# Two more PSUM banks and a longer belt in the stick-breaking attention of a three-block model

## The chip, the cores and the metric

The kernel runs on one core of a Trainium2 chip. The engines are TensorE (PE, with its weight loads shown apart as PEld), VectorE (DVE), ScalarE (ACT), GpSimd (POOL) and SyncE (SP, which issues the DMAs). The metric is the time of one execution in microseconds on the device, the median of several runs.

## What is computed

Three transformer-like blocks in a row over 1024 tokens of width 1024, in fp32. The change is in the third block, in one of its two attentions. It has 8 heads of width 64. A query at t weights the key at s < t by a sigmoid of its score, times the product of the complements of all keys between them ("stick breaking"):

```python
z = jnp.einsum('bhqd,bkhd->bhqk', qb, k) * scale
log_beta = jax.nn.log_sigmoid(z)
log_1m_beta = jnp.where(causal, jax.nn.log_sigmoid(-z), 0.0)
suffix = lax.cumsum(log_1m_beta, axis=3, reverse=True) - log_1m_beta
attn = jnp.where(causal, jnp.exp(log_beta + suffix), 0.0)
out = jnp.einsum('bhqk,bkhd->bqhd', attn, v)
# then RMS norm, output projection, LayerNorm, gated feed-forward, LayerNorm
```

## The kernel before

Instructions run on each engine in the order in which the program writes them. Waits between engines are semaphores that the framework puts in where a tile is read, or where its buffer is used again. Large matmuls (`qk`, `op`, `dn` and others) run as three matmuls of fp32r halves (hi·hi, hi·lo, lo·hi).

**Items.** The attention takes 128 queries of one head against up to 512 keys as one item. Queries 0 to 511 (`i` 0 to 3) need one item; queries 512 to 1023 (`i` 4 to 7) need two, called segments here: first the keys from 512 on, then keys 0 to 511. That is 12 items a head, 24 for a pair of heads (`p`), 96 in all. An item has three parts:

- `sb1`: scores into a PSUM bank `sb` (PE); two sigmoids from it, `f` and `beta` (ACT); a running product over `f` (the scan of L2156, DVE), a fix-up of one column of `beta`, and, for a first segment, a copy of one column as the `carry` of the second (DVE); `beta` times the shifted `f` (POOL).
- `sb2`: transposes of `beta` into a bank `sbt` (PE), copied out as `pt` (DVE, L2172).
- `sb3`: the products with the values into a bank `sbo` (PE), 64 columns wide, summed over both segments in that bank. After an item that ends its queries the sum is copied out (`ys` or `yr`, DVE, L2184) and squared (`ysq`, ACT). A two-segment sum holds its bank from the first segment's `sb3` to the second's.

**Banks.** [...] One pool `ps` has six of them and gives out a bank for each `sb`, `sbt`, `sbo`, for the projections' sums (`qk`, `op`) and for the transposes of results (`yt`). Two banks are used only by pools of other stages.

**Order.** A `Belt` writes the parts in steps: each step issues the `sb1` of a new item, the `sb2` of the item `lag` steps back, and the `sb3` of an item whose `sb2` is one or two steps old. The `Driver` mixes these steps between the matmuls of a main stream by costs that are written in the code. For the pairs p = 0 to 2, the main stream is the `qk` projection of the next pair: six matmuls, a part of a step, six matmuls, and so on. When the projections are done (around 2257 us), steps are issued without a main stream (`fsb.until`: "forced") until 80 of the 96 items are finished, with the transposes of the other attention's results (`yt`) among them. After that the output projection `op` is the main stream, and `fsb.finish` empties the belt between its two halves.

The work per step on ACT and DVE has this order: ACT `f`, `beta`, then `ysq` of the older item; DVE scan, column of `beta`, `carry`, `pt`, then `ys`.

```python
def _run(self):                       # Belt, each turn is one step
    ...
            ready = [it for n, it in self.end if n < self.n - (0 if force else 1)]
            if self.mid and self.mid[0][0] <= self.n - self.lag:
                it = self.mid.pop(0)[1]
                yield it[1](), 0.0             # sb2
                self.end.append((self.n, it))
            for it in ready:
                cost = it[2]()                 # sb3
```

`tmp` takes `f` and `beta` from a pool of eight buffers (`b3t`) until the forced steps begin, later from the general pool.

Of the kernel before, what the change touches and what calls it, by code (L numbers as in the profile page):

```python
# [9 lines left out]
F32 = mybir.dt.float32  # L10
# [4 lines left out]
PSUM = bass.MemoryType.PSUM  # L15
# [283 lines left out]
class Kernel:  # L299
# [1670 lines left out]
    def block3(self):  # L1970
        nc, a, drv, tc = self.nc, self.a, self.drv, self.tc
        from contextlib import ExitStack
        ctx = ExitStack()
        pp = ctx.enter_context(tc.tile_pool(name="b3", bufs=1))
        tp = ctx.enter_context(tc.tile_pool(name="b3t", bufs=8))
        ctx1 = ExitStack()
        kp = ctx1.enter_context(tc.tile_pool(name="b3k", bufs=4))
        roomy = []
# [64 lines left out]
        def y_put(p, n, e, branch, ssq, write):  # L2043

            own = branch == 0 and p == 3
            if own:
                yc = Y[n][:, 384 + 64 * e:448 + 64 * e]
            else:
                if e == 0:
                    YS[branch, p, n] = self.small(128, "ys")  # L2050
                yc = YS[branch, p, n][:, 64 * e:64 * e + 64]
            write(yc)
            sq = self.small(64, "ysq")
            self.act(sq, yc, AF.Square, accum=ssq[:, n, 2 * p + e:2 * p + e + 1])
            if e == 1 and not own:
                nc.sync.dma_start(out=self.yd[n][:, 512 * branch + 128 * p:512 * branch + 128 * p + 128],
                                  in_=YS.pop((branch, p, n)))
# [71 lines left out]
        def sb_unit(h, i):  # L2129
            nk = 128 * (i + 1)  # L2130
            segs = [(0, nk)] if nk <= 512 else [(512, nk - 512), (0, 512)]
            st = {"n": len(segs)}
            out = []
            for x, (k0, w) in enumerate(segs):
                out.append(((lambda x=x, k0=k0, w=w: sb1(st, h, i, x, k0, w)),
                            (lambda x=x, k0=k0, w=w: sb2(st, h, i, x, k0, w)),
                            (lambda x=x, k0=k0, w=w: sb3(st, h, i, x, k0, w))))
            return out
# [36 lines left out]
        def sb3(st, h, i, x, k0, w):  # L2175
            p, e = h // 2, h % 2
            if x == 0:
                st["po"] = self.bank("sbo")
            po, pt = st["po"], st["pt", x]
            for k in range(w // 128):  # L2180
                self.mm(po[:, 0:64], pt[:, 128 * k:128 * k + 128], V[k0 // 128 + k][:, 64 * h:64 * h + 64],
                        x == 0 and k == 0, x == st["n"] - 1 and k == w // 128 - 1)
            if x == st["n"] - 1:
                y_put(p, i, e, 0, ssb, lambda y: nc.vector.tensor_copy(out=y, in_=po[:, 0:64]))  # L2184
            return 1.7 * w

        fsw, fsb = Belt(drv, 3, 2000.0), Belt(drv, 4, 800.0)

        def q_as(branch, p, half, ps):
            q_evac(p, half, ps)  # L2190
# [96 lines left out]
        def gen_mix(half, b):  # L2287

            n0 = 4 * half
            if not b:  # L2290
                r = self.small(4, "r1")
                token_rms(r, ssb[:, n0:n0 + 4, :])
                ys = Y[n0:n0 + 4]
            else:
                r = rsw[:, n0:n0 + 4]
                ys = [self.h("yr") for _ in range(4)]
                for n in range(4):
                    nc.sync.dma_start(out=ys[n], in_=self.yd[n0 + n][:, 512:1024])
                yield 0.0, 0.0
            for n in range(4):  # L2300
                self.ts(ys[n], ys[n], r[:, n:n + 1])
            yield 0.0, 8470.0
            for c in range(4):
                ps = self.bank("yt")
                for n in range(4):
                    nc.tensor.transpose(ps[:, 128 * n:128 * n + 128], ys[n][:, 128 * c:128 * c + 128], self.ident)
                hi, lo = self.h("hhi", F32R), self.h("hlo", F32R)
                H2[0][c + 4 * b][half], H2[1][c + 4 * b][half] = hi, lo
                g = self.v("swa_norm_g_3" if b else "sb_norm_g_3", c)
                self.act(hi, ps, AF.Identity, scale=g)  # L2310
                self.stt(lo, ps, g, hi, ALU.mult, ALU.subtract)
                yield 450.0, 200.0


        roomy.append(True)
        fsb.lag = 5
        sws = [gen_mix(0, 1), gen_mix(1, 1)]
        next(sws[0])
        next(sws[1])
# [145 lines left out]
```

## Time and profile before

| | |
|---|---|
| median of 3 runs | 3154.49 us (3153.01 to 3156.83) |
| profiled execution | 3154.91 us, span 3153.1 us, mean granted TensorE clock 0.959 |
| busy, share of the span | PE 94%, PEld 80%, DVE 57%, ACT 41%, POOL 45% |
| idle of PE before the span's end | 196 us (3153.1 - 2957.1) |

The span runs from the first to the last instruction, and 1.8 us of the execution's time lie around it. The shares are means over stages that have different limits; the stick-breaking attention is a stage of some 310 us, from 2048 to 2360 us.

### The profile page before, as it was taken

The page shows a single profiled execution, that of the slowest core. Times are in us where ns is not written, and L with a number is a line of the kernel's source. Part 1 is how long each engine was busy: PE and PEld are TensorE (multiplying, and loading weights), DVE is VectorE, ACT ScalarE, POOL GpSimd, SP SyncE. Part 2 cuts the span into 40 slices and gives each one's busy share as a digit, 9 for nine tenths or more (in the row PEclk, how much of TensorE's full clock was granted, in tenths as well). Part 3 has the DMA queues.
Part 4 walks back from the last instruction along what each step waited for, and adds up shares of the span by engine and source line. Part 5 has one row for each costly group of instructions (what it writes and reads, how often), then busy time and mean ns, then how long its engine had stood idle before and what let it go on. Part 6 is the DMA issues. An engine that isn't in the chain of part 4 may idle for free. (4 is left out here: it accounts for less than half of the span.)

```text
span 3153.1 us, 41402 instructions
## 1 busy us (share of the span) xinstructions
PE 2957.1 (94%) x15188; PEld 2514.3 (80%) x15188; DVE 1808.9 (57%) x3522; ACT 1286.6 (41%) x2493; POOL 1429.0 (45%) x1008
## 2 busy tenths in 40 slices
PE   8999998999999999889998989988889899999997
PEld 7898776888878877778897778877678788888886
DVE  6443246666665579966645664566666522224556
ACT  4232224444432254466573356644443422222223
POOL 4313434777743356852214352143333477764330
PEclk9999999999999999999998989989889999999998
DMA  4101241222253221132113332100122222225321
GB/s 159 34 21 54 73 127 41 80 84 81 84 180 107 81 84 51 45 96 60 45 39 104 106 111 64 45 19 22 63 73 94 87 81 81 80 84 177 107 81 54
DMA packets 114876, 248.96 MB, mean 79 GB/s; under 512 B 19696, under 2 KB 31600, under 8 KB 114672
## 3 DMA queue, kind: packets, MB, share of 16 engines
q1 hardware_dynamic: 114384, 246.01, 23.8%
q8 instruction: 120, 1.97, 0.3%
q14 instruction: 84, 0.69, 0.1%
q10 hardware_dynamic: 288, 0.30, 0.0%
HBM read 192.52 MB, written 53.74 MB: 78 GB/s over the span
## 5 line engine op out<-in xcount | busy, mean ns | idle before, releaser
L332 POOL TENSOR_TENSOR wlo<-raw,whi 128x1024 fp32r<-128x1024 f32 x240 | 581.4, 2431 | 861.8 <-ACT whi L326 845.0
L326 ACT ACTIVATE whi<-raw 128x1024 fp32r<-128x1024 f32 x240 | 248.2, 1053 | 537.7 <-PE dn L347 284.0
L332 DVE TENSOR_TENSOR X<-dn,X 128x512 f32<-128x512 f32 (+1 forms) x312 | 209.9, 676 | 161.7 <-PE dn L347 159.5
L347 PE MATMUL dn<-ghi,whi 128*128 128x512 f32 (+1 forms) x736 | 281.4, 382 | 0.6 <-DVE X L332 0.6
L347 PE MATMUL dn<-glo,whi 128*128 128x512 f32 (+1 forms) x736 | 280.6, 381 | 0.0
L347 PE MATMUL dn<-ghi,wlo 128*128 128x512 f32 (+1 forms) x736 | 280.5, 381 | 0.0
L332 POOL TENSOR_TENSOR raw<-raw 128x512 f32<-128x512 f32 x156 | 203.0, 1301 | 12.1
L332 POOL TENSOR_TENSOR slo<-raw,shi 128x512 fp32r<-128x512 f32 x117 | 151.1, 1305 | 105.1 <-ACT shi L326 103.8
L347 PE MATMUL p<-thi,shi 128*128 128x512 f32 x468 | 185.0, 395 | 12.7 <-DVE u L1105 9.4
L332 DVE TENSOR_TENSOR v<-p,e 128x512 f32<-128x512 f32 x78 | 53.8, 690 | 243.2 <-ACT e L326 193.6
L347 PE MATMUL p<-hhi,wlo 128*128 128x512 f32 x468 | 182.4, 390 | 1.7 <-POOL wlo L332 1.7
L347 PE MATMUL p<-tlo,shi 128*128 128x512 f32 x468 | 183.6, 392 | 0.0
L347 PE MATMUL p<-thi,slo 128*128 128x512 f32 x468 | 183.4, 392 | 0.0
L347 PE MATMUL p<-hhi,whi 128*128 128x512 f32 x468 | 182.3, 390 | 0.0
L347 PE MATMUL p<-hlo,whi 128*128 128x512 f32 x468 | 182.3, 390 | 0.0
L329 DVE SCALAR_TENSOR_TENSOR t<-u,vec,t 128x512 f32<-128x512 f32 x176 | 133.0, 755 | 79.7 <-ACT t L326 74.5
L347 PE MATMUL qk<-hhi,whi 128*128 128x512 f32 x384 | 164.9, 430 | 7.9 <-ACT hhi L326 7.2
L332 POOL TENSOR_TENSOR beta<-beta,f 128x511 f32<-128x511 f32 (+3 forms) x96 | 88.4, 925 | 180.7 <-DVE beta L336 177.8
L347 PEld LDWEIGHTS dn<-ghi,whi 128*128 128x128 f32 x736 | 139.3, 189 | 28.0 <-DVE X L332 1.4
L347 PEld LDWEIGHTS dn<-ghi,wlo 128*128 128x128 f32 x736 | 139.1, 189 | 26.3
L347 PEld LDWEIGHTS dn<-glo,whi 128*128 128x128 f32 x736 | 139.2, 189 | 25.8
L347 PE MATMUL qk<-hlo,whi 128*128 128x512 f32 x384 | 156.3, 407 | 1.5 <-DVE hlo L329 1.5
(400 smaller groups left out, 8186.8 us busy)
## 6 DMA issues: line engine op xcount, KB each, us to landing
raw<-in_wall SPq DMA_DIRECT2D x240, 512.0 KB, 3.8
gd<-g SPq DMA_DIRECT2D x88, 256.0 KB, 2.1
gx<-gd SPq DMA_DIRECT2D x88, 256.0 KB, 5.1
x2d<-X SPq DMA_DIRECT2D x64, 256.0 KB, 2.0
X<-x2d SPq DMA_DIRECT2D x64, 256.0 KB, 5.3
x<-in_xT SPq DMA_DIRECT2D x16, 256.0 KB, 5.8
X<-in_xT SPq DMA_DIRECT2D x16, 256.0 KB, 4.3
T<-in_rpbx SPq DMA_DIRECT2D x8, 448.0 KB, 3.6
```

Source lines behind the costliest of these rows:

```text
L326: self.nc.scalar.activation(out=out, in_=in_, func=func, bias=bias, scale=scale, **kw)
L329: self.nc.vector.scalar_tensor_tensor(out=out, in0=in0, scalar=s, in1=in1, op0=op0, op1=op1)
L332: (eng or self.nc.vector).tensor_tensor(out=out, in0=in0, in1=in1, op=op)
L347: self.nc.tensor.matmul(out=out, lhsT=lhsT, rhs=rhs, start=start, stop=stop, skip_group_check=more)
```

## The change

Three numbers and a pool. A pool `po2` of two PSUM banks, on the two that `ps` does not have, holds the output sums of the queries with two segments; the one-segment sums stay in `ps`. The belt's lag is five in place of four, and six in place of five from the forced steps on. The pool of `f` and `beta` has ten buffers in place of eight.

```diff
-        tp = ctx.enter_context(tc.tile_pool(name="b3t", bufs=8))
+        tp = ctx.enter_context(tc.tile_pool(name="b3t", bufs=10))
+        po2 = ctx.enter_context(tc.tile_pool(name="b3p", bufs=2, space=PSUM))
...
             if x == 0:
-                st["po"] = self.bank("sbo")
+                st["po"] = (self.bank("sbo") if st["n"] == 1 else
+                            po2.tile([128, 512], F32, tag="o", name="sbo"))
...
-        fsw, fsb = Belt(drv, 3, 2000.0), Belt(drv, 4, 800.0)
+        fsw, fsb = Belt(drv, 3, 2000.0), Belt(drv, 5, 800.0)
...
         roomy.append(True)
-        fsb.lag = 5
+        fsb.lag = 6
```

Up to the stage's first transposes every engine's instructions stand as before, and no instruction is added or taken away. Inside the stage the order shifts, and waits change.

PE, first pair of heads, at the first output sum `sbo` (names with buffer numbers; the semaphores that a row waits for in brackets). Before:

```order
L2170 MATMUL sbt_18400<-ident_74,beta_18324 128x128 [waits DVE_49,Activation_49,Pool_49]
L347 MATMUL sbo_18404<-v_15723,pt_18361 128x64 [waits DVE_49,Activation_49]
L347 MATMUL sbo_18404<-v_15724,pt_18361 128x64
L347 MATMUL sbo_18404<-v_15725,pt_18361 128x64
L347 MATMUL sbo_18404<-v_15726,pt_18361 128x64
L347 MATMUL sb_18409<-ks_18157,qq_18123 128x384 [waits PE_49]
```

Now:

```order
L347 MATMUL sb_18403<-ks_18160,ql_18127 128x384
L347 LDWEIGHTS identb_15712
L347 MATMUL sb_18403<-sbmb_15713,identb_15712 128x128
L2171 MATMUL sbt_18416<-ident_74,beta_18327 128x128 [waits DVE_49,Activation_49,Pool_49]
L347 MATMUL sbo_18420<-v_15726,pt_18375 128x64 [waits DVE_49]
L347 MATMUL sbo_18420<-v_15727,pt_18375 128x64
```

The scores of the second 384-wide item (`sb_18409`, now `sb_18403`) stand ahead of this sum and not behind it, and the sum waits for its `pt` (DVE) alone, no longer for a bank that ACT reads.

ACT, where the second pair's items begin (behind the key evacuation `ks` and two weight splits `whi`). Before:

```order
L326 ACTIVATE ks<-qk 64x512 x2
L326 ACTIVATE whi<-raw 128x1024 x2
L326 ACTIVATE f<-sb 128x512
L326 ACTIVATE beta<-sb 128x512
L326 ACTIVATE f<-sb 128x512
L326 ACTIVATE beta<-sb 128x512
L326 ACTIVATE f<-sb 128x128
L326 ACTIVATE beta<-sb 128x128
L326 ACTIVATE ysq,ssb<-ys 128x64
L326 ACTIVATE f<-sb 128x512
```

Now:

```order
L326 ACTIVATE ks<-qk 64x512 x2
L326 ACTIVATE whi<-raw 128x1024 x2
L326 ACTIVATE f<-sb 128x512
L326 ACTIVATE beta<-sb 128x512
L326 ACTIVATE ysq,ssb<-ys 128x64
L326 ACTIVATE f<-sb 128x512
L326 ACTIVATE beta<-sb 128x512
L326 ACTIVATE f<-sb 128x128
L326 ACTIVATE beta<-sb 128x128
L326 ACTIVATE f<-sb 128x512
```

A square `ysq` has moved by one step; there are as many of them as before, and each still stands between the `beta` of one item and the `f` of the next.

PE, forced steps, just ahead of the first `yt`. Before:

```order
L2170 MATMUL sbt<-ident,beta 128x128 x4
L347 MATMUL sbo<-v,pt 128x64 x4
L2306 MATMUL yt<-ident,yr 128x128 x16
L347 MATMUL sb<-ks,qq 128x256
L347 MATMUL sb<-ks,ql 128x256
```

Now:

```order
L347 MATMUL sb<-ks,qq 128x256
L347 MATMUL sb<-ks,ql 128x256
L347 LDWEIGHTS identb
L347 MATMUL sb<-sbmb,identb 128x128
L2171 MATMUL sbt<-ident,beta 128x128 x4
L347 MATMUL sbo<-v,pt 128x64 x4
L2308 MATMUL yt<-ident,yr 128x128 x16
```

One more item's scores stand ahead of `yt`; in the same way one more stands ahead of the first `op`. Where `fsb.finish` empties the belt, six items are transposed one after the other in place of five.

## Rows read from the trace of the kernel before

**Rows 1.** Busy time by engine: pairs 0 to 2, forced steps, steps among `op`, after.

```profile
core 0: us, PE busy (x) PEld busy (x) DVE busy (x) ACT busy (x) POOL busy (x), PEclk, DMA share, GB/s
2054.00:2257.30 203.30, 178.20 (x1056) 148.56 (x1054) 137.47 (x298) 94.29 (x264) 82.46 (x87) 0.93 0.06 18
2257.30:2307.00 49.70, 35.55 (x183) 30.54 (x183) 34.56 (x70) 22.64 (x64) 18.26 (x16) 0.69 0.37 121
2307.00:2360.00 53.00, 49.02 (x291) 42.28 (x291) 35.98 (x73) 20.93 (x49) 19.39 (x15) 0.94 0.18 53
2360.00:2420.00 60.00, 60.00 (x289) 50.28 (x289) 37.70 (x64) 21.28 (x33) 12.56 (x6) 1.00 0.27 87
```

**Rows 2.** Groups by line, PE, 2054 to 2257.3: busy, mean ns | idle before.

```profile
L347 PE MATMUL sbo<-v,pt 128*128 128x64 f32 x400 | 56.2, 280 | 6.6 <-DVE ql L329 3.3 <-ACT beta L326 2.2 <-DVE pt L2172 0.6
...
L2170 PE MATMUL sbt<-ident,beta 128*128 128x128 f32 x200 | 35.0, 285 | 7.3 <-ACT beta L326 3.5 <-DVE pt L2172 2.2 <-DVE ks L332 1.4
L347 PE MATMUL sb<-ks,qq 128*128 128x512 f32 (+3 forms) x70 | 30.0, 429 | 10.4 <-DVE pt L2172 3.9 <-ACT beta L326 3.4 <-DVE ql L329 2.4
```

**Rows 3.** Timeline, PE, 2065 to 2069: start, us, instructions [idle before].

```profile
2065.84 0.43 PE L347 MATMUL sbo<-v,pt 128*128 128x64 f32 x2 [1.78 <-ACT beta L326]
...
2067.10 0.40 PE L347 MATMUL qk<-hhi,wlo 128*128 128x512 f32 x1
...
2068.04 0.63 PE L347 MATMUL qk<-hhi,wlo 128*128 128x512 f32 x1
```

**Rows 4.** Waits, ACT, 2054 to 2257.3: us in total, times, longest.

```profile
ACT ysq L326 <- DVE ys L2184: 76.1, 44, 4.7
ACT f L326 <- PE sb L347: 19.3, 16, 4.2
```

**Rows 5.** Waits, DVE, 2054 to 2257.3.

```profile
DVE f L2156 <- ACT f L326: 43.3, 44, 2.4
DVE ql L329 <- ACT qq L326: 12.2, 9, 1.6
...
DVE pt L2172 <- PE sbt L2170: 1.8, 2, 1.2
DVE ys L2184 <- PE sbo L347: 1.2, 2, 0.7
```

**Rows 6.** Timelines of DVE and of ACT, one step, 2249 to 2253.

```profile
2249.75 1.28 DVE L2156 TENSOR_TENSOR_SCAN f<-f,carry 128x512 f32<-128x512 f32 x1 [1.30 <-ACT f L326]
...
2251.05 0.55 DVE L2172 COPY pt<-sbt 128x384 f32<-128x384 f32 x1
2251.52 0.22 DVE L2184 COPY ys<-sbo 128x64 f32<-128x64 f32 x1
2252.63 1.28 DVE L2156 TENSOR_TENSOR_SCAN f<-f,carry 128x512 f32<-128x512 f32 x1 [0.90 <-ACT f L326]
...
2251.77 0.26 ACT L326 ACTIVATE ysq<-ys 128x64 f32<-128x64 f32 x1 [1.56 <-DVE ys L2184]
...
2252.02 0.58 ACT L326 ACTIVATE f<-sb 128x512 f32<-128x512 f32 x1
```

**Rows 7.** Timeline, DVE: the other long waits for scores, pairs 0 to 2.

```profile
2089.12 1.28 DVE L2156 TENSOR_TENSOR_SCAN f<-f,carry 128x512 f32<-128x512 f32 x1 [2.40 <-ACT f L326]
2109.62 1.28 DVE L2156 TENSOR_TENSOR_SCAN f<-f,ones 128x512 f32<-128x512 f32 x1 [1.19 <-ACT f L326]
2144.35 0.75 DVE L2156 TENSOR_TENSOR_SCAN f<-f,ones 128x256 f32<-128x256 f32 x1 [1.83 <-ACT f L326]
2179.04 1.28 DVE L2156 TENSOR_TENSOR_SCAN f<-f,carry 128x512 f32<-128x512 f32 x1 [1.97 <-ACT f L326]
```

**Rows 8.** Timelines of PE and of DVE where the forced steps begin.

```profile
2268.08 1.94 PE L347 MATMUL sbo<-v,pt 128*128 128x64 f32 x8 [4.46 <-DVE pt L2172]
...
2263.92 3.18 DVE L2156 TENSOR_TENSOR_SCAN f<-f,ones 128x512 f32<-128x512 f32 x1
```

**Rows 9.** Timeline, PE, steps among `op` and the belt's last items.

```profile
2313.43 1.11 PE L347 MATMUL sbo<-v,pt 128*128 128x64 f32 x8 [1.67 <-ACT beta L326]
...
2317.98 1.11 PE L347 MATMUL sbo<-v,pt 128*128 128x64 f32 x8 [1.26 <-DVE pt L2172]
...
2319.96 0.78 PE L2170 MATMUL sbt<-ident,beta 128*128 128x128 f32 x3 [0.51 <-POOL beta L332]
...
2355.36 1.11 PE L347 MATMUL sbo<-v,pt 128*128 128x64 f32 x8 [0.27 <-DVE pt L2172]
```

## The prediction

> **What bounds the kernel now.** I read the busy time by stretch first [rows 1], then the idle time of PE in the stage that is changed [rows 2], then what ACT and DVE wait for there [rows 4, 5], and last single steps in the timelines [rows 3, 6 to 9].
>
> Behind the stage PE is busy without a gap at the full clock (its last row) [rows 1], so what the stage gains or loses passes to the end. Within it two things stand beside each other. While the `qk` projections run (2054 to 2257.3), PE is busy for 178.2 of 203.3 us at a mean granted clock of 0.93 [rows 1]: 25.1 us idle, of which the attention's own instructions have 6.6 + 7.3 + 10.4 = 24.3 us [rows 2]. Nearly all of that is waiting for a bank, and one can see it from the names. A sum `sbo` doesn't read `beta` or `ql`, and scores `sb` don't read `pt`; an instruction that waits for such a reader waits for the bank that it empties. Only `sbo` after `pt` (0.6 us) can be for data. So the first reading is that PE is starved of banks.
>
> The second reading is less kind. In the same stretch DVE is busy for only 137.5 us, ACT for 94.3 [rows 1], and yet they hardly ever rest freely, because they wait for each other in a ring [rows 6]: DVE's scan, then `pt`, then the copy `ys` at 2251.52; ACT's square `ysq` at 2251.77, which had waited 1.56 us for that copy; behind it `f` of the next item at 2252.02, and only then the next scan, at 2252.63 after 0.90 us idle. One turn takes 2252.63 - 2249.75 = 2.88 us. PE is in this ring only where its scores, transposes or sums are late. ACT waited 76.1 us in 44 waits for DVE's copies in front of a square, against 19.3 us in 16 waits for scores [rows 4]. So most of PE's waiting for banks is waiting for a ring that sets the pace anyway; PE is ahead and has nowhere to put its results.
>
> **The change part by part.**
>
> *The two banks.* A two-segment sum kept a bank of the six across three items, and mostly two such sums were open. `qk` had another. Three were left for scores, transposes and short sums; now five are. What this can give is bounded by what lateness of PE costs the ring, not by PE's idle time. Two ways to that number. DVE waited 43.3 us in 44 waits for `f` before a scan [rows 5]. A wait that belongs to the ring is 0.90 us [rows 6], so 44 x 0.90 = 39.6 us stay and 3.7 us are lateness. The five longest waits say the same one by one: 2.40, 1.97, 1.83, 1.19 [rows 7] and 1.30 [rows 6] make 8.7 us, less 5 x 0.90 = 4.5, or 4.2 us. I take 4. To this come 1.8 us in which DVE waited for transposes and 1.2 us for sums [rows 5]. Term one: **-7 us**. Its bounds are 0 (the ring takes it all) and -19.3 us (all of ACT's waits for scores [rows 4] are on the path). I take the value by DVE, since a wait of ACT costs nothing while DVE still has a scan or a copy to do. DVE's 12.2 us for `ql` [rows 5] stay: ACT and DVE take turns there on one `qk` bank.
>
> A slower clock comes into this but is not a term of its own. [...] Of 203.3 us, 0.07 is 14 us of lost clock [rows 1]; it matters where it makes scores late, and that is in the waits counted above.
>
> *Among the `op` matmuls* PE is busy for 49.0 of 53.0 us [rows 1], so here a wait of PE does count. Two waits of `sbo`, 1.67 and 1.26 us, are for banks [rows 9]; both sums now have banks of their own, but the second then meets its `pt` sooner. The wait of 0.51 us before transposes [rows 9] stays, their banks are still in the six. Term two: **-2 us**, bounds 0 and -2.9.
>
> *The longer belt.* It removes no wait of its own in the rows: no group there is a `beta` that comes too late for its transposes, apart from parts of the 7.3 us in [rows 2], whose releasers are ACT, `pt` and `ks`, none of them POOL. In pairs 0 to 2 it only moves each `sb2`, `sb3` and `ysq` by a step, with as many squares in front of an `f` as before; I cost it at nothing there, the cover being the ring. Where steps are forced it costs: with one more item in flight, one more must be begun before the first `op`. A step of that kind takes 2.88 us [rows 6], without a main stream to fill it. It is missing later among the `op` steps, where it would have taken PE's time as well. Term three: **+1 us**, bounds 0 and +2.9. At the last emptying one more item goes from transposes to `pt` to its sum with little beside it. One such sum took 1.11 us after a wait of 0.27 us [rows 9], and a transpose group 0.78 us [rows 9] at most: up to 2.2 us, but only the wait is new, the work was only elsewhere. Term four: **+0.5 us**, bounds 0 and +2.2.
>
> *Ten buffers* for `f` and `beta` add no instruction. One more item in flight needs one more `beta`, so ten at lag five stand as eight at lag four; if that cover were missing, ACT would wait before `beta`, at up to a turn of 2.88 us each time.
>
> *What stays.* The forced steps begin with a wait of PE of 4.46 us for `pt` behind a scan that took 3.18 us in place of 1.28 [rows 8, 6], and 0.69 of the clock is granted in that stretch [rows 1]. No bank is in that chain.
>
> **Sum.** -7 - 2 + 1 + 0.5 = -7.5 us. The profiled execution took 3154.9 us, 0.4 over the median of the runs, so 3147.4 for it and **3147.0 us** for the median. All bounds on one side give -22 and +5 us, 3132 to 3160.
>
> **The rivals.**
>
> *The ring is all.* ACT's queue stays in its order, so `f` of an item comes after `ysq` of an older one however early the scores are. For it: 76.1 us against 19.3 [rows 4]. Against it: the five long waits [rows 7, 6] are at scores that came late, and DVE itself waited 3.0 us for PE [rows 5]. Term one falls to 0 to -3: 3151 to 3155 us. [...]
>
> *PE was the bound.* All 24.3 us of bank waits [rows 2] come off, and what they cost in clock does not return elsewhere: 3130 us. For it: the size, and a clock that falls after such waits [rows 3]. Against it: DVE's 137.5 us, and 39.6 + 12.2 us of waits inside the ring, leave only 14 of 203.3 us, part of which is the key evacuation. [...] The trace shows the waits, but not that they end the stage.
>
> *The longer belt costs more than the banks give.* Place: the forced steps and the last emptying. Price: 2.9 + 2.2 = 5.1 us if nothing of it is hidden, 3160 us with nothing gained. It decides when terms one and two together are under 5 us. Against it: the item is moved and not added.
>
> *The change doesn't reach the waits.* The six banks are still handed on at once, scores into the bank that the last scores left; then the same waits stand at other names. Time: 3154 us.
>
> **How the numbers follow.** The forecast, 3142 to 3151 us, has 0.50; the ring alone 0.22; PE as the bound 0.14; the belt's cost 0.08; no reach 0.06. A measurement of this kernel tells some 0.2%, 6.3 us, from no change, so faster means under 3148.2 us: about two thirds of the forecast's chance and all of the third case, 0.47. Slower means over 3160.8 us, the bad end of the fourth and what I have not seen: 0.07. The rest, 0.46, is the same. The range that leaves out no more than 2 in 10 goes from 3135 to 3156 us.
>
> **What would show it.** In the changed kernel, over the stretch of pairs 0 to 2: PE's idle time before `sb`, `sbt` and `sbo` falls from 24.3 us to about 10, what is left names `pt` for `sbo`; ACT's waits for scores fall from 19.3 us to under 8; its waits of `ysq` for `ys` stay above 65 us; DVE's waits for transposes and sums go from 3.0 us to under 1; the stretch is 7 us shorter. Among `op` the waits of `sbo` for ACT's `beta` are gone. I am wrong if ACT's waits for scores fall and the stretch doesn't shorten (the ring), if the stretch loses 15 us or more (PE), or if the stretch gains and the forced steps give it back.

## The result and the profile after

The changed kernel took 3130.95 us (median of 4 runs, 3128.46 to 3137.06) against 3153.75 us before (4 runs beside it): a ratio on record of 0.9938, interval 0.9926 to 0.9951 (the two medians by themselves give 0.9928, 22.8 us). Timed again later it took 3135.15 us, with a ratio of 0.9950 (0.9936 to 0.9963). So by these ratios it is 0.5 to 0.6% faster, 16 to 20 us, where 7.5 us were forecast. The first time lies outside the forecast's range of 3135 to 3156 us, on its good side; the second stands at its end.

The profiled execution had a span of 3129.7 us against 3153.1. To see where the 23.4 us went, I cut both executions at the same four points of the program: the first `qk` matmul of the set that runs beside pair 0, the last `qk` matmul, the first `op` matmul, and the first projection matmul behind the last sum. Windows of before (columns as in [rows 1], but these start where the work does):

```profile
2045.62:2255.81 210.19, 185.57 (x1079) 154.24 (x1079) 140.84 (x308) 99.99 (x275) 82.99 (x87) 0.92 0.07 21
2255.81:2307.03 51.22, 36.59 (x188) 31.20 (x188) 35.78 (x74) 22.84 (x64) 18.82 (x16) 0.69 0.36 117
2307.03:2359.78 52.75, 48.77 (x290) 42.03 (x290) 35.98 (x73) 20.89 (x49) 19.39 (x15) 0.94 0.17 52
2359.78:3153.10 793.32, 760.14 (x3458) 630.48 (x3457) 360.63 (x575) 238.57 (x368) 390.92 (x244) 0.98 0.28 94
```

The same windows of the changed kernel:

```profile
2042.14:2234.50 192.36, 173.96 (x1072) 143.91 (x1072) 139.07 (x307) 97.76 (x276) 85.74 (x87) 0.98 0.08 24
2234.50:2288.22 53.72, 39.36 (x198) 34.12 (x197) 37.05 (x79) 24.86 (x69) 19.82 (x17) 0.64 0.35 113
2288.22:2336.18 47.96, 46.22 (x289) 39.79 (x288) 31.37 (x70) 19.81 (x47) 18.89 (x14) 0.98 0.21 67
2336.18:3129.70 793.52, 760.06 (x3458) 630.59 (x3457) 359.91 (x575) 238.56 (x368) 390.49 (x244) 0.98 0.28 93
```

Pairs 0 to 2 lose 17.8 us, the forced steps gain 2.5, the steps among `op` lose 4.8, and what follows is unchanged (+0.2). The 3.5 us by which the first window starts earlier are no effect: up to there the program is the same, and in 16 other profiles of this study that point lies anywhere from 2040.3 to 2049.0 us.

The three groups of PE that answer to [rows 2], 2042.14 to 2234.50:

```profile
L347 PE MATMUL sbo<-v,pt 128*128 128x64 f32 x390 | 52.1, 270 | 2.8 <-DVE pt L2173 2.0 <-ACT f L326 0.6
L2171 PE MATMUL sbt<-ident,beta 128*128 128x128 f32 x199 | 33.8, 278 | 6.5 <-DVE ys L2186 3.7 <-POOL beta L332 1.2 <-DVE ql L329 0.5
L347 PE MATMUL sb<-ks,qq 128*128 128x512 f32 (+3 forms) x73 | 30.0, 411 | 8.4 <-DVE ks L332 4.2 <-ACT beta L326 3.2 <-DVE pt L2173 0.6
```

ACT's waits there (as [rows 4]), then DVE's (as [rows 5]):

```profile
ACT ysq L326 <- DVE ys L2186: 74.4, 42, 3.3
ACT f L326 <- PE sb L347: 1.8, 4, 1.1
```

```profile
DVE f L2157 <- ACT f L326: 34.2, 40, 2.0
DVE ql L329 <- ACT qq L326: 10.7, 8, 1.6
```

Read them against the busy times. PE's idle time fell by only 6.2 us (length less busy: 24.6 to 18.4); the other 11.6 us of the 17.8 are busy time of PE, which did the same work at a granted clock of 0.98 in place of 0.92. And ACT hardly waits for scores any more, while it still waits 74.4 us for `ys`.

Last the chain that ended last, in that stretch, by line (`issue` is time in which the profile shows nothing that the engine waited for); before first, with three of its longest pieces (start, us, what):

```profile
by line: DVE f L2156 18.1%; PE qk L347 17.4%; DVE pt L2172 9.2%; PE sb L347 8.6%; PE sbo L347 8.0%; ACT f L326 8.0%; issue 6.8%; ACT qq L326 4.4%; PE sbt L2170 4.0%; ACT ysq L326 4.0%; DVE ql L329 2.9%; DVE beta L336 2.4%; DVE ks L332 2.3%;
...
2085.22 2.67 PE qk L347 x6
...
2124.40 2.56 PE qk L347 x6
2140.13 2.56 PE qk L347 x6
```

Changed:

```profile
by line: DVE f L2157 27.6%; DVE pt L2173 13.0%; issue 8.8%; ACT f L326 7.5%; ACT ysq L326 7.0%; PE qk L347 4.4%; PE sbo L347 4.3%; DVE beta L336 3.9%; ACT qq L326 3.6%; DVE ql L329 3.5%; DVE ks L332 2.9%; DVE ys L2186 2.8%; PE sb L347 2.5%;
```

Summed over all its pieces, the chain of before held 81 us of PE and 129 us of DVE, ACT and issue; that of the changed kernel 26 and 166. Six `qk` matmuls took 1.44 us at the full clock (before, from 2052.27 us, granted 1.00); the three pieces above ran at a granted clock of 0.50, 0.50 and 0.52. Each PE piece of before, times one less the granted clock in it, gives 14.9 us of lost clock on the chain; the changed kernel has none in this profile, and 5.1 us in a second one.

### The profile page after: what moved, and what is told of

Its sections match the earlier page's. It is cut to its first block, busy times and chain, and to the rows that moved or that the text cites. A ratio compares the mean times of both kernels' runs of the same rounds, so it can differ in the third digit from the quotient of the medians.

```text
span 3129.7 us, 41397 instructions
## 1 busy us (share of the span) xinstructions
PE 2941.2 (94%) x15188; PEld 2499.6 (80%) x15188; DVE 1803.3 (58%) x3522; ACT 1284.8 (41%) x2493; POOL 1432.9 (46%) x1008
## 5 line engine op out<-in xcount | busy, mean ns | idle before, releaser
L347 PE MATMUL op<-hhi,wlo 128*128 128x512 f32 x384 | 153.2, 399 | 4.0 <-POOL wlo L332 4.0
```

The lines of the kernel that those rows point to most:

```text
L347: self.nc.tensor.matmul(out=out, lhsT=lhsT, rhs=rhs, start=start, stop=stop, skip_group_check=more)
```

## The experiments

Each run has its ratio to the kernel before, timed beside it. A stretch is read from one execution; the differences of a run's stretches, summed, agree with its ratio within 5 us, so a difference of 1 or 2 us between two stretches tells little. The theories that they tell apart: **PE is the bound** (the rival that gave 3130 us). **The ring of DVE and ACT is the bound** (what my forecast leaned on). **The clock** is a price of its own: waits of PE bring it down (behind the wait of [rows 3] the granted clock of before went from 0.99, 2067.1 to 2067.5 us, to 0.50, 2067.5 to 2070.0), and that lies on the chain. **The lag** does it, which I had costed at nothing.

### The parts apart

Banks alone:

```diff
+        po2 = ctx.enter_context(tc.tile_pool(name="b3p", bufs=2, space=PSUM))
-                st["po"] = self.bank("sbo")
+                st["po"] = (self.bank("sbo") if st["n"] == 1 else
+                            po2.tile([128, 512], F32, tag="o", name="sbo"))
```

> The two banks alone, belts at the lags of before (4, then 5), eight buffers. If PE with its clock sets the stage (each bank wait is paid by PE and a lower clock follows it): most of the gain is here, 3133 to 3141 us, and in the stretch of pairs 0 to 2 (210.2 us before, 192.4 in the changed kernel) PE's idle time falls from 24.5 to about 15 us and the granted clock rises from 0.93 to 0.97 or more. If the ring of DVE and ACT sets it: at most 4 us, 3150 us or more, whatever PE's idle time does. If the gain comes from the longer lag: within 3 us of before.

Measured 3139.93 us, ratio 0.9964 (0.9953 to 0.9976), about 11 us. The stretches:

```profile
2040.29:2241.15 200.86, 182.85 (x1079) 152.08 (x1079) 140.49 (x308) 98.03 (x275) 83.92 (x87) 0.93 0.07 22
2241.15:2292.70 51.55, 35.80 (x189) 30.84 (x188) 36.17 (x74) 23.23 (x65) 18.83 (x16) 0.70 0.35 117
2292.70:2341.21 48.51, 46.70 (x291) 40.56 (x290) 35.70 (x73) 20.70 (x49) 19.40 (x15) 0.97 0.20 60
```

The banks take 9.3 us off pairs 0 to 2 and 4.2 off the `op` steps. The time is the one expected if PE with its clock sets the stage, but the signs are not: the clock stayed at 0.93 where 0.97 was to come, and PE's idle time fell to 18.0 us and not to 15. What did fall are the waits of DVE for `f`, before first, then with the banks, and its waits for transposes and sums (1.8 and 1.2 us) are gone:

```profile
DVE f L2156 <- ACT f L326: 45.0, 46, 2.4
```

```profile
DVE f L2157 <- ACT f L326: 40.2, 42, 3.2
```

Lags alone:

```diff
-        tp = ctx.enter_context(tc.tile_pool(name="b3t", bufs=8))
+        tp = ctx.enter_context(tc.tile_pool(name="b3t", bufs=10))
-        fsw, fsb = Belt(drv, 3, 2000.0), Belt(drv, 4, 800.0)
+        fsw, fsb = Belt(drv, 3, 2000.0), Belt(drv, 5, 800.0)
-        fsb.lag = 5
+        fsb.lag = 6
```

> The lags alone (5, then 6, ten buffers), with the two-segment sums still in the six banks. If the banks bring the gain: 3150 to 3160 us, since one more item in flight keeps nothing in a bank longer but sets sums later; PE's idle time in pairs 0 to 2 stays over 20 us. If the lag brings it (transposes and sums that come a step later no longer meet a reader that is late): 3133 to 3142 us with banks as before. If both are needed: between, 3142 to 3150 us.

Measured 3157.26 us, ratio 1.0020 (1.0011 to 1.0029): slower by some 6 us, with 214.5 us in pairs 0 to 2 (4.3 more than before) and 30.3 of them idle on PE. The two parts do not add: -11 and +6 make -5, and together they gave -16 to -20. The longer lag costs with six banks and pays with eight.

Five forced items in place of six in the changed kernel (`fsb.lag = 5` at the second place):

> The changed kernel with five items in place of six where steps are forced. In the profiles the forced stretch took 51.2 us before and 53.7 in the changed kernel, the steps among op 52.8 and 48.0; with the banks alone they took 51.6 and 48.5. If the longer forced belt costs what the prediction gave it (its third term, +1, at most 2.9 us): 1 to 3 us less than the changed kernel, and a forced stretch near 51.5 us. If its price comes back among op: within 1 us of the changed kernel. The stretch of pairs 0 to 2 stays at 190 to 196 us either way; if the gain there needs the six, 198 us or more.

Measured 3131.78 us, ratio 0.9929 (0.9917 to 0.9942), not told apart from the changed kernel by its time; by the stretches:

```profile
2043.61:2236.38 192.77, 176.50 (x1072) 146.50 (x1072) 138.46 (x305) 97.43 (x272) 84.78 (x87) 0.96 0.08 23
2236.38:2288.12 51.74, 37.23 (x196) 31.92 (x195) 35.27 (x76) 23.86 (x68) 18.78 (x16) 0.69 0.36 117
2288.12:2336.62 48.50, 46.45 (x291) 40.35 (x290) 35.71 (x73) 20.59 (x49) 19.41 (x15) 0.98 0.19 56
```

So the sixth forced item costs 2.0 us in the forced steps and gives 0.5 back among `op`, and the lag of five in pairs 0 to 2 is worth about 8 us beside the banks (200.9 to 192.8).

Ten buffers beside the banks, with the lags of before:

> The two banks with ten buffers for f and beta, but the lags of before (4, then 5): the run with the banks alone with one number changed. That run had a ratio of 0.9964 and a stretch of 200.9 us, the changed kernel with five forced items 0.9929 and 192.8 us. If the ten buffers are what the longer lag brought: a ratio near 0.993 and 190 to 196 us. If the lag itself does it: near 0.9964 and 198 to 203 us.

Measured 3138.93 us, ratio 0.9965 (0.9952 to 0.9979):

```profile
2040.31:2242.38 202.07, 182.95 (x1079) 152.24 (x1079) 140.54 (x307) 97.84 (x275) 82.97 (x87) 0.93 0.07 21
```

This run and the one with five forced items differ in one number, the lag in pairs 0 to 2. Their stretches are 202.1 and 192.8 us, and the intervals of their ratios (0.9952 to 0.9979, 0.9917 to 0.9942) stand apart. The buffers do nothing; the lag does it.

Six items in place of five, and twelve buffers:

> The changed kernel with six items between scores and transposes in pairs 0 to 2 in place of five, and twelve buffers. If the lag helps because results have more time before they are used: the same as with five or a little less, 3126 to 3134 us, a ratio of 0.992 to 0.994. If it helps because it sets other kinds of items beside each other in one step (the items come in a period of six, so that six sets scores and transposes of the same kind beside each other): another mean per kind of step than with five, and a time that may be 5 us or more off in either direction.

Measured 3140.09 us, ratio 0.9965 (0.9952 to 0.9978), 197.8 us in pairs 0 to 2. More time before results are used is not the reason, or six would give at least what five gives. From the starts of the scans, a period of six items (two first segments, a short item, two second segments, a short item) takes 16.9 us at lag four (with the banks), 16.2 at five and 16.6 at six, with other kinds of items slow in each: the second short item of a period (its scan to the next) 3.80, 3.28 and 3.25 us, the first of the two leading segments 1.86, 2.90 and 2.38. That fits the second reading, that the lag sets other items beside each other in a step. The scans of the second segments (`f<-f,carry`) show what it changes, at lag four, five and six:

```profile
L2157 DVE TENSOR_TENSOR_SCAN f<-f,carry 128x512 f32<-128x512 f32 x24 | 31.5, 1311 | 19.1 <-ACT f L326 19.0
```

```profile
L2157 DVE TENSOR_TENSOR_SCAN f<-f,carry 128x512 f32<-128x512 f32 x24 | 32.0, 1331 | 10.0 <-ACT f L326 9.9
```

```profile
L2157 DVE TENSOR_TENSOR_SCAN f<-f,carry 128x512 f32<-128x512 f32 x24 | 36.8, 1531 | 0.2
```

Their waits for ACT fall from 19.0 to 9.9 us and to nothing, those of all other scans rise from 21.1 to 24.3 and 33.6 us. In sum DVE waits 40.2, 34.2 and 33.6 us for `f`, so six loses nothing by waits. It loses by the scans themselves: the 72 scans of pairs 0 to 2 took 79.8, 78.7 and 84.5 us, and the 5.8 us more from five to six are as much as the stretch is longer (5.4 us). Of the 72, 13 at five and 25 at six took over a tenth more than the shortest of their width, and each of these ran beside an instruction of POOL, as the second of these two did and the first did not (lag six):

```profile
2147.59 1.28 DVE L2157 TENSOR_TENSOR_SCAN f<-f,carry 128x512 f32<-128x512 f32 x1
2149.04 1.09 POOL L332 TENSOR_TENSOR beta<-beta,f 128x511 f32<-128x511 f32 x1 [2.96 <-DVE beta L336]
2149.62 1.59 DVE L2157 TENSOR_TENSOR_SCAN f<-f,carry 128x512 f32<-128x512 f32 x1
```

By these rows five is the best since it takes waits away and sets few more scans beside POOL's products. That is read from the traces; no run moved POOL's work to test it.

### What is the bound, before and after

A third of the main projections' matmuls left out beside pairs 0 to 2, in the kernel before and in the changed one:

```diff
-            self.mm(ps, whi[:, c], hlo[k][half], False, False)
+            if not light:
+                self.mm(ps, whi[:, c], hlo[k][half], False, False)
...
-                    yield from self.gemm_a(ps, ws[w], half)
+                    yield from self.gemm_a(ps, ws[w], half, light=p > 0)
```

> The kernel before with a third of the main projections' matmuls left out while pairs 0 to 2 run (the low part of the activations, 96 matmuls of some 0.235 us at the full clock, 22.6 us of PE; the output lacks that product), with the same order of everything else. If PE's work sets the stretch: 17 to 25 us less, 3129 to 3137 us. If the ring sets it: PE's idle time grows by nearly what its busy time loses, and the stretch of 210.2 us loses under 6 us, 3148 us or more. Between: PE sets it where projections stand between belt steps, the ring where steps follow each other, about 10 us.

> The changed kernel with the same third of the main projections' matmuls left out while pairs 0 to 2 run (96 matmuls, 22.6 us of PE; the output lacks that product). If the ring is the bound of the changed kernel: 3126 to 3134 us, and PE's idle time grows by what its work loses. If PE is: 3108 to 3116 us.

Measured on before: 3147.57 us, ratio 0.9993 (0.9982 to 1.0004). On the changed kernel: 3131.79 us, ratio 0.9936 (0.9922 to 0.9949), the same as the changed kernel itself. First before, then changed:

```profile
2045.36:2251.33 205.97, 171.79 (x983) 141.54 (x983) 141.33 (x308) 99.38 (x275) 83.90 (x87) 0.89 0.07 22
```

```profile
2044.13:2235.74 191.61, 160.98 (x976) 131.85 (x976) 138.54 (x304) 96.66 (x269) 84.71 (x87) 0.94 0.07 22
```

Of 22.6 us less work for PE, 4.2 us came off this stretch of before and 0.8 of the changed kernel. PE's idle time and its slower clock took the rest: 24.6 us idle became 34.2, 18.4 became 30.6. The clock fell with the work (0.92 to 0.89, 0.98 to 0.94), so PE's busy time lost only 13.8 and 13.0 us. The amount of PE's work is not the bound, in the changed kernel not at all. Its lateness, by waits for banks and by its clock, is another matter.

The square behind the next item's sigmoids, in pairs 0 to 2, in the kernel before and in the changed one (`squares()` issues what the list `late` holds and empties it):

```diff
-            self.act(sq, yc, AF.Square, accum=ssq[:, n, 2 * p + e:2 * p + e + 1])
+            ac = ssq[:, n, 2 * p + e:2 * p + e + 1]
+            if branch == 0 and p < 3:
+                late.append((sq, yc, ac))
+            else:
+                self.act(sq, yc, AF.Square, accum=ac)
...
             self.act(b[:, 0:w], out, AF.Sigmoid)
+            squares()
```

> The kernel before with one thing changed: in pairs 0 to 2 ACT squares a finished output only behind the next item's two sigmoids, so the ring from DVE's copy over ACT's square to the next item's sigmoid is broken; banks and lags as before. If the ring sets the pace of the stretch: ACT's 74.7 us of waits for that copy and most of DVE's 45 us of waits for the sigmoid go, and the time falls by 10 us or more, to 3143 us or less. If PE sets it: the waits of ACT and DVE change, PE's idle time stays over 18 us and the time within 5 us of before, 3149 to 3158 us.

> The changed kernel, with ACT's square of a finished output put behind the next item's two sigmoids in pairs 0 to 2 (as in the earlier run on the kernel before, which gained some 13 us). In the changed kernel DVE, ACT and the issue between them make up 166 of the 192 us of the chain in that stretch, PE 26. If the ring of DVE and ACT is now the bound: 8 us or more less, 3123 us or under. If the banks and the square took away the same waits, so that nothing is left to gain: 3127 to 3134 us.

Measured on before: 3136.94 us, ratio 0.9960 (0.9946 to 0.9974), about 13 us, and 198.2 us in pairs 0 to 2. ACT's waits there:

```profile
ACT f L326 <- PE sb L347: 68.6, 43, 4.2
...
ACT ysq L326 <- DVE ys L2196: 3.0, 10, 0.4
```

The 74.7 us in front of squares are gone as expected, but ACT now waits for scores in their place (20.5 us before), and DVE's waits for `f` fall only from 45.0 to 30.5 us, where most of them were to go. With the ring broken and six banks, PE comes late.

On the changed kernel: 3110.16 us, ratio 0.9870 (0.9857 to 0.9884), some 41 us under before. Its stretch:

```profile
2045.80:2220.57 174.77, 169.06 (x1072) 144.61 (x1072) 147.47 (x306) 100.33 (x273) 84.77 (x87) 0.97 0.08 24
```

PE is busy for 169 of 174.8 us, and the chain names it, as one would expect where PE is the bound (no run took work from PE here):

```profile
by line: PE qk L347 28.3%; PE sbo L347 20.7%; PE sb L347 14.9%; DVE f L2169 13.0%; PE sbt L2183 9.8%; DVE pt L2185 3.6%; issue 2.0%; ACT qq L326 1.9%; ACT f L326 1.7%; DVE ql L329 1.6%; DVE beta L336 0.8%; ACT beta L326 0.6%; DVE ys L2198 0
```

The same with the banks but the lags of before:

> The kernel before with the two banks and with the late square, but with its lags (4, then 5) and eight buffers. If what the longer lag gives beside the banks is slack in the ring, the late square gives the same slack and the lag is not needed: 3108 to 3116 us, as the changed kernel with late squares (3110 us). If the lag gives something of its own (transposes and sums that no longer wait for results of the step before): 3118 to 3128 us.

Measured 3109.48 us, ratio 0.9859 (0.9844 to 0.9874):

```profile
2042.96:2214.89 171.93, 167.14 (x1079) 143.01 (x1079) 147.92 (x308) 100.88 (x275) 84.92 (x87) 0.99 0.09 26
```

Where the ring is broken, the longer lag gives nothing.

### The clock

Transposes that nothing reads, in front of 17 instructions before which PE waited, in the kernel before (`FILL` holds how many, 3 to 15, and `idle` is a bank that has no other use):

```diff
+        def fill(part):
+            for _ in range(FILL.get((part, count[part]), 0)):
+                nc.tensor.transpose(idle[:, 0:128], self.ident, self.ident)
+            count[part] += 1
```

> The kernel before, six banks and lags 4 and 5, with one thing added: in front of the 17 instructions at which PE waited 0.5 us or more in pairs 0 to 2 (23.4 us in all), transposes of the identity into an unused bank, some 0.9 of each wait long, that nothing reads. They give no bank and no result earlier; PE is only not idle. If the slow clock that follows those waits is what costs (14.9 us of lost clock lie on the chain that ends last in the stretch): the granted clock there rises from 0.92 to 0.97 or more, and the time falls by 6 to 15 us, to 3136 to 3145 us. If the clock only fills time in which PE would have waited: 3148 to 3155 us. If the added work itself lies in the way: over 3155 us.

Measured 3140.65 us, ratio 0.9961 (0.9949 to 0.9974):

```profile
2044.53:2245.86 201.33, 188.84 (x1216) 158.36 (x1216) 140.27 (x308) 99.34 (x275) 83.04 (x87) 0.99 0.07 22
```

137 useless instructions, 17.8 us of PE's time, make the stretch 8.9 us shorter. On its chain 2.4 us of lost clock are left of 14.9. DVE's waits for `f` fall from 45.0 us to nearly the 40.2 that the banks left, and its waits for transposes and sums are gone, as with the banks:

```profile
DVE f L2167 <- ACT f L326: 40.7, 45, 2.0
```

ACT still waits 16.6 us for scores (20.5 before, 9.7 with the banks). So before, the clock was a price, and it made most of PE's lateness as far as that reached DVE. Banks and fill take away the same waits of DVE; they were not run together.

The changed kernel again:

> The changed kernel again, for a closer ratio and a second profile. 3128 to 3134 us; in pairs 0 to 2 a granted clock of 0.96 or more and a stretch of 190 to 196 us, if the fewer falls of the clock belong to the kernel; a clock near 0.93 and 200 us or more, if the first profile was a lucky one.

Measured 3135.15 us, ratio 0.9950 (0.9936 to 0.9963), with a clock of 0.95 and 193.9 us in pairs 0 to 2. Between its two profiles lost clock (busy time times one less the clock) is some 3 and 9 us, and the stretch differs by 1.6; three other runs with the same code in pairs 0 to 2 took 192.7 to 193.8 us at 0.96 or 0.97. In the changed kernel most of a fall of the clock is absorbed.

The same fill in the forced steps of the changed kernel, first with 38 transposes, then with 60, before the longest wait:

> The changed kernel; in front of seven sums of the forced stretch and the first op steps, before which PE waited 13 us for transposed scores, transposes of the identity into columns of the sum's own bank that nothing reads, for some 0.9 of each wait. Nothing comes earlier by itself. In the changed kernel 8.0 us of lost clock lie on the chain that ends last in that stretch, after a wait of 6.2 us. If the clock is what costs there: 4 to 8 us less than the changed kernel, and a granted clock of 0.85 or more in place of 0.64. If DVE and ACT pace that stretch whatever PE's clock is: within 2 us.

> The run that filled PE's waits in the forced stretch, with 60 transposes in place of 38 before the longest: they followed each other at 0.113 us, so 38 of them took 4.31 of 6.9 us, and the clock had fallen by the time the sum began. If the clock is what costs there: 4 to 8 us less than the changed kernel, a ratio of 0.990 to 0.992, and the lost clock on the chain of that stretch falls from 8.0 us to under 3. If DVE and ACT pace it: a ratio of 0.993 to 0.995 with the clock up.

The first: 3132.83 us, ratio 0.9939 (0.9927 to 0.9952). Nothing follows from it, since the 38 transposes were over after 4.31 us and the clock fell in the 2.55 us of waiting that were left. The second: 3130.28 us, ratio 0.9935 (0.9921 to 0.9950), with the clock up:

```profile
2235.43:2286.59 51.16, 41.84 (x296) 36.82 (x295) 36.75 (x79) 23.89 (x69) 19.67 (x17) 0.90 0.36 119
```

The lost clock on the chain of that stretch fell from 8.0 to 1.5 us, and the stretch from 53.7 to 51.2. The time does not tell it from the changed kernel, so this is the second case: with the clock up, others pace the stretch. What came onto the chain in its place:

```profile
by line: DVE f L2159 17.0%; DMA yr<-yd 15.6%; POOL wlo L332 11.0%; issue 7.7%; DVE pt L2175 7.6%; DVE yr L336 6.5%; PE yt L2313 6.4%; DVE hlo L329 4.9%; ACT f L326 4.4%; PE sbo L347 4.2%; ACT ysq L326 3.8%; SPq L2305 2.4%; POOL beta L332 2.
```

### Towards a better version

Late squares in all four pairs, first in the changed kernel with the 38-transpose fill, then with the banks alone:

> The changed kernel with late squares in all four pairs and with the transposes of the run with the forced stretch filled. If the ring and the clock are two prices that add: 3110 us (late squares in pairs 0 to 2) less 4 to 8 for the clock of the forced stretch and 1 to 4 for its ring, 3098 to 3106 us. If the two are one: 3108 to 3114 us.

> The two banks and late squares in all four pairs, with the lags and buffers of before: the candidate for the best version. With late squares in pairs 0 to 2 it was 3109.5 us, ratio 0.9859, with 50.1 us in the forced stretch; late squares there too took that stretch from 52.3 to 47.2 us in the version at lags 5 and 6. If that carries over: a ratio of 0.984 to 0.986, 3104 to 3109 us. If the forced stretch at five items has no ring left: 0.986, 3109 us.

Measured 3109.91 us, ratio 0.9868 (0.9854 to 0.9881), and 3107.97 us, ratio 0.9865 (0.9851 to 0.9879). The first is the time expected if ring and clock were one price, but its fill is the one that did not hold the clock, so it doesn't tell the two cases apart. Late squares in the fourth pair take the forced steps from 50.1 to 47.7 us (banks, lags of before), which the times do not tell from nothing. The best version is the two banks, late squares and the old lags, at 3108 to 3110 us: 1.3 to 1.4% under before, 0.7 to 0.9% under the change.

The stretch of pairs 0 to 2 in all that matter (idle is length less busy; the chain's shares are sums of its pieces; two profiles of the same order of work, banks alone and banks with ten buffers, differ by 40 us in PE's share, since the chain takes one of several near ties, so only large differences are read):

```
kernel                     us     PE busy  idle  clock  chain: PE  others
before                     210.2  185.6    24.6  0.92   81         129
lags alone                 214.5  184.2    30.3  0.92   100        115
banks alone                200.9  182.9    18.0  0.93   11         190
banks, ten buffers         202.1  183.0    19.1  0.93   51         151
changed                    192.4  174.0    18.4  0.98   26         166
changed, again             193.9  178.3    15.6  0.95   27         167
before, filled             201.3  188.8    12.5  0.99   38         164
before, PE lighter         206.0  171.8    34.2  0.89   53         153
changed, PE lighter        191.6  161.0    30.6  0.94   14         177
before, late squares       198.2  181.9    16.3  0.93   117        82
changed, late squares      174.8  169.1    5.7   0.97   130        45
banks, late squares        171.9  167.1    4.8   0.99   106        67
```

## Why the prediction was too small

**The two readings.** I had put them as rivals, PE starved of banks or a ring that sets the pace. Both were true in turn. The chain of before passes between PE and the ring, and relieving one side alone gave 11 to 13 us: PE by the banks 0.9964, PE by the clock 0.9961, the ring 0.9960. Banks and ring together gave 41 to 44 us (0.9870 with the longer lag, 0.9859 without), where the two alone sum to some 24. Here two paths that took turns for want of slack between them did not hide each other's time, and untying both gave more than the two are worth one by one.

**Term one, the banks in pairs 0 to 2: right.** -7 was forecast; the banks alone measure -9.3 (-8.1 with ten buffers). The way over DVE's lateness held too: its waits for `f` were to fall to 39.6 us and came to 40.2. The clock belonged in the waits, as I had said, but I had it as a side matter: filling PE's waits took nearly the same waits from DVE.

**The longer lag in pairs 0 to 2, costed at nothing: the step that failed.** I wrote that it "only moves each `sb2`, `sb3` and `ysq` by a step" with "the cover being the ring". It is worth 8 us of the stretch beside the banks; without them the longer lags cost 4 us there (6 by the time). The error lies in taking the ring as 0.90 us a turn, whatever stands in it: at lag five a period of six items is 0.7 us shorter (twelve periods, 8 us), and DVE's waits for `f` fall to 34.2 us, under the 39.6 that I had called part of the ring. The lag lines up different items, and the wait in front of scans with a carry halves; with the ring broken the lag is worth nothing. This step is most of the miss: 8 of the 12 to 13 us by which the stretches fell further than forecast.

**Term two, among `op`: mis-sized.** -2 with a bound of -2.9; the banks alone give -4.2 against the profile of before. Some of that lies in that one profile: in three runs whose `op` steps are those of before (late squares, lighter PE, fill) they took 51.2 to 51.5 us, and against these the banks give 2.7 to 3.0. I had counted the waits, 2.9 us, and not that PE's busy time also falls: 48.8 to 46.7 us for the same instructions (290 and 291 in the records), with the clock from 0.94 to 0.97. The waits of `sbo` went as forecast; they name `pt` now, 0.98 and 0.38 us. The wait of 0.51 us before transposes was to stay, as one for a bank, and is gone: [rows 9] names POOL's `beta` for it, which the transposes read, so it was for data. With the banks alone a wait of 1.37 us before other transposes, for `pt`, came up.

**Terms three and four, the longer forced belt:** +1 and +0.5. The sixth forced item costs 2.0 us in the forced steps and gives 0.5 back among `op`, where the last emptying lies: +1.5 forecast, some +1.5 measured. Term four by itself is not told apart.

**The ten buffers, costed at nothing:** beside the banks they are nothing. At lag five the cover has a small gap: ACT waits 4.0 us before `beta` for POOL (0.5 before; 1.9 in the second profile). **The forced steps' start** "stays": it does, and is longer. Timeline of the changed kernel's PE:

```profile
2246.92 0.69 PE L347 MATMUL sbo<-v,pt 128*128 128x64 f32 x2 [6.20 <-DVE pt L2173]
```

**The rivals.** "PE was the bound" gave 3130 us and came nearest in number, for a wrong reason: taking 22.6 us of work from PE gains nothing that can be told, before (0.9993, 0.9982 to 1.0004) or in the changed kernel, and PE still waits 18 us in the stretch. "The ring is all" was half true before, and is what bounds the changed kernel. Lost clock in pairs 0 to 2, taken over all of PE's busy time there (busy time times one less the granted clock), is some 15 us before; filling took all but some 2 of them away and returned 8.9 us in the stretch. In the changed kernel, where little of PE is on the chain, some 6 us more of lost clock came with 1.6 us. Both times the stretch changed by less than the lost clock did.

**What would show it:** ACT's waits for scores under 8 us (1.8), `ysq`'s over 65 (74.4), DVE's for transposes and sums under 1 us (no row left), `sbo` behind `beta` among `op` gone: all as said. PE's idle time before `sb`, `sbt` and `sbo` "to about 10" stayed at 17.7, and the stretch lost 17.8 us in place of 7. I had written that 15 us or more would mean PE; the lighter PE shows that this sign was badly chosen.

## What to carry to other kernels

Where the chain passes back and forth between an engine and a ring of others, don't ask which of the two is the bound: neither is, and each loses what the other's lateness costs. Price slack there by relieving one side at a time and then both, and look in the chain at which clock the engine's pieces ran. A lag that seems only to move work sets other items beside each other and is not free in either direction; more of it is not better (six gave less than five). An operation that stands in an engine's queue ahead of the next item's first one, and waits, is cheaper to move than two banks are to find, and here it was worth as much (0.9960 against 0.9964).

## What the runs showed of the hardware that was not expected

Matmuls that nothing reads, 17.8 us of them in place of waits, made a kernel 0.39% faster, by keeping TensorE's granted clock at 0.99 in place of 0.92 in the stretch. In the forced steps of the changed kernel the clock fell at 2239 us (0.99 before, 0.50 behind), in a wait of 1.82 us, and after the wait of 6.20 us that followed TensorE ran at a granted clock of 0.50 from 2246.9 to about 2263 us although it had no gap there. In the traces read for it, scans of DVE took longer only beside an instruction of POOL: at lag six 25 of 72 took over a tenth more than the shortest of their width, 1.59 us for 1.28 in the case shown, all of them beside one, while 2 ran beside one and were not longer (12 at lag five). In the run with 38 of them, at a granted clock of 1.00, transposes of 128x128 f32 issued one behind the other took 0.113 us each, together 4.31 us.
